# Two trunk layers of a diffusion backbone: the FFN's gate and up products by Strassen's seven products

## The chip, the cores and the metric

The kernel runs on one core of a Trainium2 chip. A core has TensorE (PE, matrix products; PEld is its weight loads), VectorE (DVE), ScalarE (ACT) and GpSimd (POOL); SyncE (SP) issues most DMAs. The metric is device time in microseconds of one launch. The kernel before takes 1474.19 us, the median of three runs (1473.52 to 1476.16).

## The reference, cut to what matters

640 tokens (128 of a prompt, 512 of a sample) of width 1024 pass two layers. Layer 0 mixes by attention and a state-space scan, layer 1 by pooling. Each layer ends with the same dense FFN, and each of its two halves has a norm ahead and a gated residual behind it:

```python
D_FF = 2816
def swiglu(h, w_gate, w_up, w_down):
    return (jax.nn.silu(h @ w_gate) * (h @ w_up)) @ w_down

for l in range(2):
    ...                                    # mixer, residual
    fp = swiglu(modulate(xp, norm_pre_ffn[l], shf_p, scf_p), ffn_w_gate[l], ffn_w_up[l], ffn_w_down[l])
    xp = xp + gf_p * rmsnorm(fp, norm_post_ffn[l])   # and the same for xs
```

Everything is float32.

## The kernel before, in words

**Products.** A float32 product is made of three fp32r matmuls: both operands are split into a rounded high part and a low part (x minus high), and high x high, high x low and low x high are summed in PSUM (mm3, lines 87 to 93; the three groups L91, L92, L93 of the profile). ACT makes each high part, DVE or POOL each low part. For weights this is `unit` (lines 79 to 85): a DMA of 128 x 1024 into a `raw` buffer (a ring of four), `wh` by ACT, `wl` by DVE.

**FFN.** The width of 2816 is 22 tiles (ft) of 128. Gate and up of one ft: `wproj` (line 382) and `whalf` (line 375) run 8 k-blocks x 3 matmuls over each half of 320 tokens: 24 matmuls of 320 columns into one PSUM bank. ACT applies Silu to the gate (L386), DVE multiplies by up (L389), ACT and POOL split the result into `ah` and `al` (L390, L391). The ft are taken in parts of 2, 4, 4, 4, 4, 4 (PARTS); behind each part the down product of that part is added to `y` in SBUF: per token tile tt (five of 128) and half dh (512 columns) 3 matmuls of 512 columns per ft, and one DVE addition (L446; ACT's copy L444 in the first part).

**Start of an FFN.** The tiles tt leave the mixer one by one: post-norm and residual (post_half L339, L340, postnorm L354), pre-norm (L300, L303 or L305), eight PE transposes (L315), evacuation with scale and shift (L320 on DVE, L322 on ACT), split into `hh` and `hl` (L328, L329). The first part uses a cut at 384 tokens: PE can run on tiles 0 to 2 while tiles 3 and 4 (called tails) are finished.

**Background.** The residual gates come from a product of one vector with `w_mod`. `mod_gate_mac` does it on DVE: 16 multiply-adds of 512 columns (L269) per half of a gate. Three gates of two halves, 96 multiply-adds, are mixed into the FFNs through `bg()`, which runs one step between products.

**Order.** Every engine runs its own instructions in order. A scheduler lays that order when the program is built; a queued instruction waits for its inputs and holds all behind it on its engine.

Of the kernel before, what the change touches and what calls it, by code (L numbers as in the profile page):

```python
# [9 lines left out]
F32 = mybir.dt.float32  # L10
F32R = mybir.dt.float32r
# [16 lines left out]
CUT = 384  # L28
SCALE = (64 + 32) ** -0.5
PARTS = [2, 4, 4, 4, 4, 4]  # L30
KEYS = 768
LAG = 2
BAL = ((0, 0, 4), (0, 0, 0), (1, 0, 0))
# [14 lines left out]
class Net:  # L48
# [205 lines left out]
    def mod_gate_mac(self, gt, l, j, half, gain):  # L254
# [20 lines left out]
        for v in range(2):  # L275
# [9 lines left out]
            nc.vector.tensor_tensor(gt[:, v, c0 : c0 + 512], out, gb, ALU.mult)  # L285
            yield

    def mod_gate(self, pool, l, j, gain, mac=True):
        gt = pool.tile([P, 2, D], F32, tag="G", name=self.name("G"))
        f = self.mod_gate_mac if mac else self.mod_gate_half  # L290
        self.bgq += [f(gt, l, j, half, gain) for half in range(2)]
        return gt

    def prenorm(self, x, tt, ab, hh=None, hl=None, full=None, bal=(0, 0, 0)):
# [12 lines left out]
        def tr():  # L307
            f = full
            if f is None:
                f = self.work.tile([P, KC, P], F32, tag="full", name=self.name("full"), bufs=1)  # L310
            for q in range(2):
# [21 lines left out]
    def post_half(self, y, dst, tt, g, half, ss=None):  # L333
# [4 lines left out]
        dump = self.work.tile([P, 512], BF16, tag="dump", name=self.name("dump"), bufs=1)  # L338
# [43 lines left out]
    def ffn(self, l, xs, hh, hl, g, fp, mk_y, tails, after):  # L382
        nc, t = self.nc, self.t

        def gate(cs, s, og):
            nc.scalar.activation(s[:, cs], og, AF.Silu)  # L386

        def up(s, cs, ou, ah, al):
            nc.vector.tensor_tensor(s[:, cs], s[:, cs], ou, ALU.mult)  # L389
            nc.scalar.activation(ah[:, cs], s[:, cs], AF.Copy)  # L390
            nc.gpsimd.tensor_tensor(al[:, cs], s[:, cs], ah[:, cs].bitcast(F32), ALU.subtract)  # L391

        def tiles():
            s = fp.tile([P, TOK], F32, tag="sg", name=self.name("sg"), bufs=2)
            ah = fp.tile([P, TOK], F32R, tag="ah", name=self.name("ah"), bufs=4)
            al = fp.tile([P, TOK], F32R, tag="al", name=self.name("al"), bufs=4)
            return s, ah, al

        ft = 0
        for pi, cnt in enumerate(PARTS):  # L400
            lastp = pi == len(PARTS) - 1
            at = []
            if pi == 0:
                us = [
                    self.unit(t[w][l, f], 1024, nc.gpsimd)
                    for f in range(cnt) for w in ("w_gate", "w_up")
                ]
# [1059 lines left out]
```

## Time and profile before

| | |
|---|---|
| time, median of 3 | 1474.19 us |
| span of the profiled execution, first to last instruction | 1471.5 us |
| PE busy | 1408.8 us, 96% |
| DVE / ACT / POOL busy | 745.0 (51%) / 534.6 (36%) / 240.1 (16%) us |
| mean granted TensorE clock | 0.983 of full |
| read from HBM | 146.14 MB, 102 GB/s over the span |

The profiled execution shows its span; 1474.19 - 1471.5 = 2.7 us of the median lie around it. Busy times of PE are modelled and overlap, so the distance between the starts of matmuls tells more than their length. An engine's idle time matters where it holds another up.

### The profile page before, as it was taken

To read this page: it belongs to the slowest core of one execution; us is meant where nothing else is said; L and a number is where in the kernel's file an instruction comes from. 1 tells how busy PE (TensorE), PEld (TensorE's weight loads), DVE (VectorE), ACT (ScalarE), POOL (GpSimd) and SP (SyncE) were. 2 spreads that over 40 slices of the span, in tenths; PEclk is the share of its full clock that TensorE was granted. 3 is DMA by queue.
4 is the path that set the end of the run, shared out by engine and by line. 5 is a ranking of instruction groups with operands and counts; after the bars stand their busy time and mean duration, and the time that the engine had idled before them with its cause. 6 is when DMAs were issued, how large, how long until landed. Compare 5 with 4: busy or idle time off the path is not lost.

```text
span 1471.5 us, 20386 instructions
## 1 busy us (share of the span) xinstructions
PE 1408.8 (96%) x8256; PEld 1220.3 (83%) x8256; DVE 745.0 (51%) x1200; ACT 534.6 (36%) x1003; POOL 240.1 (16%) x243
## 2 busy tenths in 40 slices
PE   5999999999998999999999999769999999999998
PEld 2888764677566999998989999659998989999996
DVE  4755548777747425636633232895255432322326
ACT  3544635744225432221222222676321222222223
POOL 0000144344303101011211102211120101101010
PEclk9999999999999999999999999989999999999999
DMA  9433445500351223334422222101242312222211
GB/s 366 134 129 126 142 145 189 188 30 1 114 171 59 80 72 129 112 109 137 137 72 72 72 86 72 58 29 65 86 131 93 129 57 87 73 86 72 72 44 72
DMA packets 46217, 150.74 MB, mean 102 GB/s; under 512 B 5606, under 2 KB 9190, under 8 KB 46124
## 3 DMA queue, kind: packets, MB, share of 16 engines
q1 hardware_dynamic: 40176, 143.48, 28.6%
q10 hardware_dynamic: 5948, 5.97, 1.3%
q8 instruction: 65, 1.06, 0.3%
q14 instruction: 28, 0.23, 0.1%
HBM read 146.14 MB, written 3.29 MB: 102 GB/s over the span
## 4 chain that ended last, share of the span: by engine, by line
PE 87%; DVE 6%; ACT 3%; issue 2%; DMA 2%; POOL 0%; ACTq 0%; DVEq 0%; POOLq 0%
PE ps L91 25%; PE ps L92 25%; PE ps L93 25%; PE ps L175 3%; PE ps L1001 1%; DVE xs L354 1%; DVE hl L329 1%; PE ps L809 1%; PE ps L963 1%; PE ps L983 1%; PE ps L984 1%; PE ps L986 1%; PE ps L985 1%; DVE pw L1102 1%; ACT full L322 0%
## 5 line engine op out<-in xcount | busy, mean ns | idle before, releaser
L91 PE MATMUL ps<-hh,wh 128*128 128x320 f32 (+3 forms) x1616 | 501.2, 310 | 7.5 <-DVE hh L328 7.1
L92 PE MATMUL ps<-hl,wh 128*128 128x320 f32 (+3 forms) x1616 | 498.7, 309 | 2.6 <-DVE hl L329 2.6
L93 PE MATMUL ps<-hh,wl 128*128 128x320 f32 (+3 forms) x1616 | 498.4, 309 | 0.0
L84 DVE TENSOR_TENSOR wl<-raw,wh 128x1024 fp32r<-128x1024 f32 (+1 forms) x153 | 189.3, 1239 | 284.2 <-ACT wh L83 283.9
L91 PEld LDWEIGHTS ps<-hh,wh 128*128 128x128 f32 (+1 forms) x1616 | 303.1, 188 | 20.0 <-DVE hh L328 7.3
L83 ACT ACTIVATE wh<-raw 128x1024 fp32r<-128x1024 f32 (+1 forms) x161 | 170.1, 1058 | 411.1 <-PE ps L92 204.6
L92 PEld LDWEIGHTS ps<-hl,wh 128*128 128x128 f32 (+1 forms) x1616 | 303.0, 188 | 4.6 <-DVE hl L329 3.6
L93 PEld LDWEIGHTS ps<-hh,wl 128*128 128x128 f32 (+1 forms) x1616 | 302.9, 187 | 0.4 <-DVE wl L84 0.3
L391 POOL TENSOR_TENSOR al<-sg,ah 128x320 fp32r<-128x320 f32 (+2 forms) x88 | 112.2, 1274 | 726.6 <-ACT ah L390 726.6
L92 PE MATMUL ps<-wl,ah 128*128 128x512 f32 x440 | 172.9, 393 | 0.0
L91 PE MATMUL ps<-wh,ah 128*128 128x512 f32 x440 | 172.3, 392 | 0.0
L93 PE MATMUL ps<-wh,al 128*128 128x512 f32 x440 | 171.6, 390 | 0.0
L389 DVE TENSOR_TENSOR sg<-sg,ps 128x320 f32<-128x320 f32 (+2 forms) x88 | 42.8, 487 | 160.3 <-PE ps L93 160.3
L446 DVE TENSOR_TENSOR y<-y,ps 128x512 f32<-128x512 f32 x100 | 68.5, 685 | 104.0 <-PE ps L93 103.9
L91 PEld LDWEIGHTS ps<-wh,ah 128*128 128x128 f32 x440 | 82.6, 188 | 18.3
L93 PEld LDWEIGHTS ps<-wh,al 128*128 128x128 f32 x440 | 82.6, 188 | 18.1
L92 PEld LDWEIGHTS ps<-wl,ah 128*128 128x128 f32 x440 | 82.7, 188 | 16.8
L390 ACT ACTIVATE ah<-sg 128x320 fp32r<-128x320 f32 (+2 forms) x88 | 40.8, 463 | 110.3 <-DVE sg L389 110.2
L386 ACT ACTIVATE sg<-ps 128x320 f32<-128x320 f32 (+2 forms) x88 | 37.7, 428 | 98.5 <-PE ps L93 98.5
L269 DVE SCALAR_TENSOR_TENSOR macc<-raw,silc,macc 128x512 f32<-128x512 f32 x84 | 62.4, 792 | 5.3 <-DMA raw<-in_w_mod 5.3
L175 PE MATMUL ps<-raw,silc 128*32 128x512 f32 x224 | 55.5, 613 | 0.3 <-DMA raw<-in_w_mod 0.3
L315 PE MATMUL ps<-cm,junk 128*128 128x128 f32 x120 | 18.8, 308 | 19.9 <-DVE junk L305 11.8
(305 smaller groups left out, 1629.1 us busy)
## 6 DMA issues: line engine op xcount, KB each, us to landing
raw<-in_w_mod SPq DMA_DIRECT2D x80, 512.0 KB, 3.4
raw<-in_w_gate SPq DMA_DIRECT2D x44, 512.0 KB, 3.2
raw<-in_w_up SPq DMA_DIRECT2D x44, 512.0 KB, 3.3
raw<-in_w_down SPq DMA_DIRECT2D x44, 512.0 KB, 3.3
mraw<-in_w_mod SPq DMA_DIRECT2D x16, 512.0 KB, 6.4
raw<-in_w_xbc SPq DMA_DIRECT2D x8, 512.0 KB, 4.3
raw<-in_w_out SPq DMA_DIRECT2D x8, 512.0 KB, 4.7
x<-in_x_sample SPq DMA_DIRECT2D x4, 512.0 KB, 9.2
```

Source lines behind the costliest of these rows:

```text
L83: self.nc.scalar.activation(h[:, :n], x[:, :n], AF.Copy)
L84: (eng or self.nc.vector).tensor_tensor(l[:, :n], x[:, :n], h[:, :n].bitcast(F32), ALU.subtract)
L91: mm(out, ah, bh, start=first and i == 0, stop=False)
L92: mm(out, ah, bl, start=False, stop=False)
L93: mm(out, al, bh, start=False, stop=last and i == n - 1)
L175: nc.tensor.matmul(out[32 * g : 32 * g + 32], self.silc[:, kc], x[:, k2 * 512 : k2 * 512 + 512], start=kc < 4, stop=kc >= 4,)
L269: nc.vector.scalar_tensor_tensor(acc[:, v], x[:, k2 * 512 : k2 * 512 + 512], self.silc[:, kc, v : v + 1], acc[:, v] if kc else bb, op0=ALU ...
L386: nc.scalar.activation(s[:, cs], og, AF.Silu)
L389: nc.vector.tensor_tensor(s[:, cs], s[:, cs], ou, ALU.mult)
L390: nc.scalar.activation(ah[:, cs], s[:, cs], AF.Copy)
L391: nc.gpsimd.tensor_tensor(al[:, cs], s[:, cs], ah[:, cs].bitcast(F32), ALU.subtract)
L446: nc.vector.tensor_tensor(yd, yd, out, ALU.add)
```

## The change

Gate and up of a pair of ft (256 columns) become one 2x2 block product: the contraction is cut in two halves of 512, the columns in two ft, the tokens in two halves of 320. Strassen's scheme in the form of Winograd needs seven block products instead of eight, and sums of blocks ahead of and behind them. A block product is 4 k-blocks x 3 matmuls of 320 columns.

- Weights (`Matrix`): per pair and matrix two `raw` tiles, four POOL subtractions of 512 columns (`adds`), and four splits: a (the raw tile itself, products p1, p2), c (p5, p6), b (p7, p3), d (p4, 512 columns).
- Activations (`Halves`): `take` splits tokens 0 to 319 as before (`a1`). From tile 3 on `pair` forms the four sums S1 to S4 of the halves (three on DVE, one on POOL) and splits them and the block A22 (`a2`). p1 and p2 read only a1, all other products a2.
- Results: the PSUM tile A is carried through p1, p6, p7, p4 and copied out by ACT in between; B holds p5 and p3; DVE adds them up in SBUF.
- Down product: per pair of ft, five tiles of six matmuls, placed between products by `d()`, each with a DVE addition; `d()` also runs one background step. The last two pairs are kept for the end.
- The residual x and the three gates go to scratch in DRAM and are read back at the end of each FFN, which frees SBUF for a2.

```diff
-PARTS = [2, 4, 4, 4, 4, 4]
+NPAIR = NFT // 2
...
-BAL = ((0, 0, 4), (0, 0, 0), (1, 0, 0))
...
+    def split(self, pool, tag, x, eng=None):
+        n = x.shape[1]
+        h = pool.tile([P, n], F32R, tag="h" + tag, name=self.name("h" + tag))
+        l = pool.tile([P, n], F32R, tag="l" + tag, name=self.name("l" + tag))
+        self.nc.scalar.activation(h, x, AF.Copy)
+        (eng or self.nc.vector).tensor_tensor(l, x, h.bitcast(F32), ALU.subtract)
+        return h, l
...
+    def take(self, tt):
+        nc = self.net.nc
+        if tt < 3:
+            cs = slice(tt * P, min(tt * P + P, HB))
+            h, l = (a[:, :, cs] for a in self.a1)
+            x = self.f[:, :, cs]
+            nc.vector.tensor_copy(h, x)
+            nc.vector.tensor_tensor(l, x, h.bitcast(F32), ALU.subtract)
+        if tt == 3:
+            self.pair(0, 64)
+        if tt >= 3:
+            self.pair(tt * P - HB, P)
+
+    def pair(self, c0, n):
+        nc = self.net.nc
+        cs = slice(c0, c0 + n)
+        fa, fb = self.f[:, :, cs], self.f[:, :, HB + c0 : HB + c0 + n]
+        t = self.tmp.tile([P, 4, 4, P], F32, tag="st", name=self.net.name("st"))[:, :, :, 0:n]
+        h, l = self.a2
+        s1, s2 = t[:, self.S1], t[:, self.S2]
+        nc.vector.tensor_tensor(s1, fb[:, 0:4], fb[:, 4:8], ALU.add)
+        nc.gpsimd.tensor_tensor(t[:, self.S3], fa[:, 0:4], fb[:, 0:4], ALU.subtract)
+        nc.vector.tensor_tensor(s2, s1, fa[:, 0:4], ALU.subtract)
+        nc.vector.tensor_tensor(t[:, self.S4], fa[:, 4:8], s2, ALU.subtract)
+        for i in range(2):
+            b = slice(2 * i, 2 * i + 2)
+            self.split(
+                h[:, b, :, cs].rearrange("p s k c -> p (s k) c"),
+                l[:, b, :, cs].rearrange("p s k c -> p (s k) c"),
+                t[:, b].rearrange("p s k c -> p (s k) c"), nc.vector,
+            )
+        self.split(h[:, self.A22, :, cs], l[:, self.A22, :, cs], fb[:, 4:8], nc.gpsimd)
...
+    def load(self):
+        self.ra = self.net.raw(self.src[2 * self.pair])
+        self.rb = self.net.raw(self.src[2 * self.pair + 1])
+
+    def adds(self):
+        g = self.net.nc.gpsimd
+        lo, hi = slice(0, 512), slice(512, 1024)
+        self.q = self.fr.tile([P, 1024], F32, tag="q", name=self.net.name("q"))
+        self.t4 = self.fr.tile([P, 512], F32, tag="t4", name=self.net.name("t4"))
+        g.tensor_tensor(self.q[:, lo], self.rb[:, lo], self.ra[:, lo], ALU.subtract)
+        g.tensor_tensor(self.q[:, hi], self.rb[:, hi], self.q[:, lo], ALU.subtract)
+        g.tensor_tensor(self.rb[:, lo], self.rb[:, hi], self.rb[:, lo], ALU.subtract)
+        g.tensor_tensor(self.t4, self.ra[:, hi], self.q[:, hi], ALU.subtract)
...
+        terms = [t for k in range(4) for t in ((wh, bh, k), (wh, bl, k), (wl, bh, k))]
+        for n, (x, z, k) in enumerate(terms):
+            mm(out, x[:, k], z[:, k], start=first and n == 0, stop=n == len(terms) - 1, skip_group_check=True)
...
+        def p1(self):
+            self.A = net.pt([P, HB])
+            self.m.product(self.A, 1, A, True, True)
+            nc.scalar.activation(self.blk(0, 0), self.A, AF.Copy)
+
+        def p2(self):
+            c = net.pt([P, HB])
+            self.m.product(c, 2, A, True, True)
+            nc.vector.tensor_tensor(self.blk(0, 0), self.blk(0, 0), c, ALU.add)
+            self.act(0, 0)
+
+        def p6(self):
+            self.m.product(self.A, 6, A, False, True)
+            nc.scalar.activation(self.blk(1, 0), self.A, AF.Copy)
+
+        def p5(self):
+            self.B = net.pt([P, HB])
+            self.m.product(self.B, 5, A, True, True)
+
+        def p7(self):
+            self.m.product(self.A, 7, A, False, True)
+            nc.scalar.activation(self.blk(1, 1), self.A, AF.Copy)
+            nc.vector.tensor_tensor(self.blk(1, 1), self.blk(1, 1), self.B, ALU.add)
+
+        def p4(self):
+            self.m.product(self.A, 4, A, False, True)
+            self.act(0, 1, self.A)
+
+        def p3(self):
+            self.m.product(self.B, 3, A, False, True)
+            nc.vector.tensor_tensor(self.blk(1, 0), self.blk(1, 0), self.B, ALU.add)
+            if self.g is None:
+                nc.scalar.activation(self.s[:, 1], self.s[:, 1], AF.Silu)
             else:
-                us = [[dunit(j, dh) for j in range(cnt // 2)] for dh in range(2)]
-                lag = []
-                for tt in range(NT):
-                    y2 = [y[:, tt, dh * 512 : dh * 512 + 512] for dh in range(2)]
-                    down(tt, 0, us[0])
-                    self.bg()
-                    u = self.post_tile()
-                    ss = self.post_half(y2[0], u[0], tt, g, 0)
-                    down(tt, 1, us[1])
-                    self.bg()
-                    if len(lag) >= LAG:
-                        lag.pop(0)()
-                    self.post_half(y2[1], u[1], tt, g, 1, ss)
-                    if l == 0:
-                        self.postnorm(u, ss, xs[:, tt])
-                        lag.append(after(tt))
-                    else:
-                        self.postnorm(u, ss, xs[:, tt], lambda cs: after(tt, cs))
-            ft += cnt
-        return lag
+                nc.vector.tensor_tensor(self.g.s[:, 1], self.g.s[:, 1], self.s[:, 1], ALU.mult)
...
+        def d():
+            if fill:
+                down_add(fill.pop(0), up, [(prev, wdn)], p == 1)
+            net.bg()
+
+        if nx and n != 0:
+            nx.load()
+        if n >= 2:
+            w.p1()
+            w.p2()
+        if final and up:
+            last[1, 0] = net.split(fr, "a", down_load(NPAIR - 1, 0), None)
+        w.p6()
+        d()
+        w.p5()
+        if nx and n != 0:
+            nx.a()
+        w.p7()
+        if nx:
+            nx.adds()
+        d()
+        if nx:
+            nx.c()
+        if final and up:
+            last[0, 1] = net.split(fr, "c", down_load(NPAIR - 2, 1), None)
+        w.p4()
+        if up:
+            at = [out_split(wg, 0)]
+        d()
+        w.p3()
+        if up:
+            at.append(out_split(wg, 1))
+        if nx:
+            nx.b()
+            nx.d()
+        d()
+        d()
+        if up:
+            if final:
+                last[1, 1] = net.split(fr, "b", down_load(NPAIR - 1, 1), None)
+                last["at"] = (prev, at)
+            prev = at
+        if nx and 1 <= n and (n + 1) // 2 < NPAIR - 1:
+            wdn = net.split(fr, "w", down_load((n + 1) // 2 - 1, (n + 1) % 2), None)
...
-            lag.append(net.prenorm(xs[:, tt], tt, ab_ffn, hh, hl, bal=BAL[0]))
+            x = xq.pop(0)
+            net.postnorm([y[:, tt, 0:512], u[1]], sss[tt], x)
+            nc.sync.dma_start(xd[0, tt], x)
+            if tt + 3 < NT:
+                x_in(tt + 3)
+            lag.append(net.prenorm(x, tt, ab_ffn, sink=A, bal=(0, 4)))
...
+    def x_back(pl, k):
+        xs = pl.tile([P, NT, D], F32, name=net.name("xs"))
+        for tt in range(NT):
+            nc.sync.dma_start(xs[:, tt], xd[k, tt])
+        return xs
```

**Where instructions move.** On DVE at the start of the first FFN, from the evacuation of tile 3 to that of tile 4 (`full` is the evacuated tile, `xs` the residual, `sg` the gate), before:

```order
L320 TENSOR_SCALAR full_4490<-ps_4500,mv_418,mv_417 128x128
L354 SCALAR_TENSOR_TENSOR xs<-ymix,r_4416,xs 128x512
L354 SCALAR_TENSOR_TENSOR xs<-junk_4411,r_4416,xs 128x512
L320 TENSOR_SCALAR full_4490<-ps_4500,mv_418,mv_417 128x128 x3
L328 CAST hh_3853<-full_4490 128x8x128
L329 TENSOR_TENSOR hl_3854<-full_4490,hh_3853 128x8x128
L99 RECIPROCAL r_4425<-sd_4424 128x1
L305 TENSOR_SCALAR junk_4421<-xs,r_4425 128x1024
L389 TENSOR_TENSOR sg_4458<-sg_4458,ps_4511 128x384
L320 TENSOR_SCALAR full_4539<-ps_4549,mv_418,mv_417 128x128 x4
L328 CAST hh_3853<-full_4539 128x8x128
L329 TENSOR_TENSOR hl_3854<-full_4539,hh_3853 128x8x128
```

After, the last tile's part (`st` the sums, `a2l` low parts of a2, `la`, `lw` low parts of weights for later products):

```order
L433 TENSOR_TENSOR st_4535<-full_3857 128x512
L526 TENSOR_TENSOR sg_4490<-sg_4490,sg_4491 128x320
L435 TENSOR_TENSOR st_4535<-st_4535,full_3857 128x512
L90 TENSOR_TENSOR la_4752<-raw_4721,ha_4751 128x1024
L436 TENSOR_TENSOR st_4535<-full_3857,st_4535 128x512
L411 TENSOR_TENSOR a2l_4463<-st_4535,a2h_4462 128x8x128
L90 TENSOR_TENSOR lw_4825<-raw_4822,hw_4824 128x1024
L411 TENSOR_TENSOR a2l_4463<-st_4535,a2h_4462 128x8x128
L433 TENSOR_TENSOR st_4593<-full_3857 128x512
L435 TENSOR_TENSOR st_4593<-st_4593,full_3857 128x512
L436 TENSOR_TENSOR st_4593<-full_3857,st_4593 128x512
L411 TENSOR_TENSOR a2l_4463<-st_4593,a2h_4462 128x8x128 x2
```

One cast and one low part per tile have become three sums and two low parts, and the low parts of weights stand between them.

On ACT at the start of the second FFN, before (`full` again the evacuations of tiles 3 and 4):

```order
L98 ACTIVATE sd_8841<-ss_8839,eps 128x1
L322 ACTIVATE full_8902<-ps_8903,mv_1564,mv_1565 128x128
L303 ACTIVATE junk_8838<-xs,r_8842 128x1024
L322 ACTIVATE full_8902<-ps_8903,mv_1564,mv_1565 128x128 x3
L322 ACTIVATE full_8902<-ps_8912,mv_1564,mv_1565 128x128 x4
L390 ACTIVATE ah_8871<-sg_8870 128x384
L322 ACTIVATE full_8951<-ps_8952,mv_1564,mv_1565 128x128 x4
L322 ACTIVATE full_8951<-ps_8961,mv_1564,mv_1565 128x128 x4
L386 ACT_TABLE_LOAD
```

After, from the first high parts of a2 (`ha`, `hw` are high parts of later weights):

```order
L410 ACTIVATE a2h_9127<-st_9189 128x8x64 x2
L410 ACTIVATE a2h_9127<-full_8730 128x4x64
L410 ACTIVATE a2h_9127<-full_8730 128x4x128
L523 ACT_TABLE_LOAD
L523 ACTIVATE sg_9155<-sg_9155 128x320
L410 ACTIVATE a2h_9127<-st_9200 128x8x128 x2
L531 ACTIVATE sg_9156<-ps_9226 128x320
L335 ACTIVATE full_8730<-ps_9240,mv_1571,mv_1572 128x128 x4
L335 ACTIVATE full_8730<-ps_9249,mv_1571,mv_1572 128x128 x4
L89 ACTIVATE ha_9416<-raw_9386 128x1024
L410 ACTIVATE a2h_9127<-full_8730 128x4x128
L89 ACTIVATE hw_9489<-raw_9487 128x1024
L410 ACTIVATE a2h_9127<-st_9258 128x8x128 x2
```

The evacuation of tile 4 (ps_9240, ps_9249) now stands behind the table load and four high parts, and behind it come two high parts of weights ahead of tile 4's own.

On DVE in the stretch where a gate is computed, before (`macc` is the gate's sum, `wl` low parts):

```order
L389 TENSOR_TENSOR sg_4938<-sg_4938,ps_5030 128x320
L269 SCALAR_TENSOR_TENSOR macc_5340<-raw_5341,silc,macc_5340 128x512
L84 TENSOR_TENSOR wl_5248<-raw_5245,wh_5247 128x1024
L269 SCALAR_TENSOR_TENSOR macc_5340<-raw_5375,silc,macc_5340 128x512 x4
L269 SCALAR_TENSOR_TENSOR macc_5340<-raw_5409,silc,macc_5340 128x512
L84 TENSOR_TENSOR wl_5312<-raw_5309,wh_5311 128x1024
L269 SCALAR_TENSOR_TENSOR macc_5340<-raw_5409,silc,macc_5340 128x512 x2
L389 TENSOR_TENSOR sg_5061<-sg_5061,ps_5128 128x320
L269 SCALAR_TENSOR_TENSOR macc_5340<-raw_5409,silc,macc_5340 128x512
L389 TENSOR_TENSOR sg_5061<-sg_5061,ps_5153 128x320
L84 TENSOR_TENSOR wl_5318<-raw_5315,wh_5317 128x1024
```

After, in one matrix of layer 0:

```order
L275 SCALAR_TENSOR_TENSOR macc_5390<-raw_5391,silc,bb_5385 128x512
L526 TENSOR_TENSOR sg_5208<-sg_5208,sg_5399 128x320
L90 TENSOR_TENSOR la_5470<-raw_5400,ha_5469 128x1024
L590 TENSOR_TENSOR y<-y,ps_5446 128x512
L275 SCALAR_TENSOR_TENSOR macc_5390<-raw_5391,silc,macc_5390 128x512 x2
L275 SCALAR_TENSOR_TENSOR macc_5390<-raw_5503,silc,macc_5390 128x512
L90 TENSOR_TENSOR lc_5506<-q_5487,hc_5505 128x1024
L550 TENSOR_TENSOR sg_5399<-sg_5399,ps_5456 128x320
L275 SCALAR_TENSOR_TENSOR macc_5390<-raw_5503,silc,macc_5390 128x512
L590 TENSOR_TENSOR y<-y,ps_5493 128x512
L275 SCALAR_TENSOR_TENSOR macc_5390<-raw_5503,silc,macc_5390 128x512 x2
L526 TENSOR_TENSOR sg_5208<-sg_5208,ps_5404 128x320
```

The multiply-adds are the same ones; between them now stand the low parts of four weight blocks instead of two units, the block additions and the additions to y.

## Rows read from the trace of the kernel before

**Rows 1.** Page, part 1: busy time, share and instructions of each engine.
```profile
PE 1408.8 (96%) x8256; PEld 1220.3 (83%) x8256; DVE 745.0 (51%) x1200; ACT 534.6 (36%) x1003; POOL 240.1 (16%) x243
```

**Rows 2.** Groups by shape, TensorE: count | busy us, mean ns | idle.
```profile
L91 PE MATMUL ps<-hh,wh 128*128 128x320 f32 x1472 | 455.6, 310 | 0.0
```

**Rows 3.** Timeline, TensorE in layer 0's FFN: start, length in us.
```profile
560.33 0.31 PE L91 MATMUL ps<-hh,wh 128*128 128x320 f32 x1
...
563.41 0.31 PE L91 MATMUL ps<-hh,wh 128*128 128x320 f32 x1
...
599.62 0.39 PE L91 MATMUL ps<-wh,ah 128*128 128x512 f32 x1
...
603.97 0.39 PE L92 MATMUL ps<-wl,ah 128*128 128x512 f32 x1
```

**Rows 4.** Windows of the FFN: stretch, busy us and count of each engine.
```profile
640.00:720.00 80.00, 80.00 (x476) 74.72 (x475) 48.77 (x66) 18.93 (x29) 10.38 (x7) 1.00 0.37 124
720.00:800.00 80.00, 80.00 (x477) 74.88 (x477) 26.62 (x34) 19.05 (x29) 10.09 (x8) 1.00 0.26 87
```

**Rows 5.** Groups by shape, VectorE (DVE).
```profile
L84 DVE TENSOR_TENSOR wl<-raw,wh 128x1024 fp32r<-128x1024 f32 x152 | 188.4, 1241 | 284.2 <-ACT wh L83 283.9
L446 DVE TENSOR_TENSOR y<-y,ps 128x512 f32<-128x512 f32 x100 | 68.5, 685 | 104.0 <-PE ps L93 103.9
L269 DVE SCALAR_TENSOR_TENSOR macc<-raw,silc,macc 128x512 f32<-128x512 f32 x84 | 62.4, 792 | 5.3 <-DMA raw<-in_w_mod 5.3
L389 DVE TENSOR_TENSOR sg<-sg,ps 128x320 f32<-128x320 f32 x80 | 38.9, 487 | 146.8 <-PE ps L93 146.8
L279 DVE TENSOR_TENSOR modl<-macc,modh 128x512 fp32r<-128x512 f32 x12 | 8.2, 684 | 0.3
```

**Rows 6.** Groups by shape, GpSimd (POOL).
```profile
L391 POOL TENSOR_TENSOR al<-sg,ah 128x320 fp32r<-128x320 f32 x80 | 102.0, 1275 | 668.8 <-ACT ah L390 668.8
L1018 POOL TENSOR_TENSOR cal<-a,cah 128x512 fp32r<-128x512 f32 x4 | 5.2, 1296 | 11.8 <-ACT cah L1017 11.8
L1232 POOL TENSOR_TENSOR csl<-zs,csh 128x640 fp32r<-128x640 f32 x4 | 6.1, 1554 | 20.3 <-ACT csh L1231 20.3
```

**Rows 7.** Groups by shape, ScalarE (ACT).
```profile
L83 ACT ACTIVATE wh<-raw 128x1024 fp32r<-128x1024 f32 x160 | 169.4, 1060 | 411.1 <-PE ps L92 204.6 <-PE ps L93 115.7 <-issue 70.0
L322 ACT ACTIVATE full<-ps,mv,mv 128x128 f32<-128x128 f32 x60 | 22.9, 461 | 11.9 <-PE ps L315 5.9 <-DVE r L99 3.7 <-DVE hl L329 2.4
L98 ACT ACT_TABLE_LOAD x6 | 7.7, 1283 | 0.1
```

**Rows 8.** Timeline before the first FFN: VectorE, then GpSimd.
```profile
459.22 0.75 DVE L354 SCALAR_TENSOR_TENSOR xs<-ymix,r,xs 128x512 f32<-128x512 f32 x1
...
466.46 2.86 DVE L354 SCALAR_TENSOR_TENSOR xs<-ymix,r,xs 128x512 f32<-128x512 f32 x1
...
469.25 2.82 DVE L354 SCALAR_TENSOR_TENSOR xs<-junk,r,xs 128x512 f32<-128x512 f32 x1
...
475.79 3.38 DVE L329 TENSOR_TENSOR hl<-full,hh 128x1024 fp32r<-128x1024 f32 x1
...
465.50 8.79 POOL L84 TENSOR_TENSOR wl<-raw,wh 128x1024 fp32r<-128x1024 f32 x3 [58.68 <-ACT wh L83]
...
475.69 2.39 POOL L84 TENSOR_TENSOR wl<-raw,wh 128x1024 fp32r<-128x1024 f32 x1 [1.41 <-ACT wh L83]
```

**Rows 9.** Timeline of the same start, TensorE.
```profile
479.22 0.69 PE L92 MATMUL ps<-hl,wh 128*128 128x384 f32 x1 [1.00 <-DVE hl L329]
...
480.34 0.52 PE L92 MATMUL ps<-hl,wh 128*128 128x384 f32 x1
...
484.28 0.34 PE L92 MATMUL ps<-hl,wh 128*128 128x384 f32 x1
```

**Rows 10.** Timeline before the second FFN: TensorE, then VectorE.
```profile
999.96 0.44 PE L92 MATMUL ps<-hl,wh 128*128 128x384 f32 x1 [1.23 <-DVE hl L329]
...
1001.58 1.41 DVE L354 SCALAR_TENSOR_TENSOR xs<-junk,r,xs 128x512 f32<-128x512 f32 x2
```

More of the change, by code (lines that the diff above doesn't have):

```diff
@@ L307, in tr @@
         def tr():
-            f = full
-            if f is None:
-                f = self.work.tile([P, KC, P], F32, tag="full", name=self.name("full"), bufs=1)
+            f = sink.f[:, :, tt * P : tt * P + P] if full is None else full
             for q in range(2):
@@ new lines, with __init__, second, begin @@
+class Halves:
+    S2, S1, S3, S4, A22 = range(5)
+    def __init__(self, net, pool):
+        self.net = net
+        self.a1 = [pool.tile([P, KC, HB], F32R, name=n) for n in ("a1h", "a1l")]
+    def second(self, pool, tmp):
+        self.a2 = [pool.tile([P, 5, 4, HB], F32R, name=self.net.name(n)) for n in ("a2h", "a2l")]
+        self.tmp = tmp
+    def begin(self, pool):
+        self.f = pool.tile([P, KC, TOK], F32, name=self.net.name("full"))
+    def split(self, h, l, x, eng):
+        nc = self.net.nc
+        nc.scalar.activation(h, x, AF.Copy)
+        eng.tensor_tensor(l, x, h.bitcast(F32), ALU.subtract)
+    def take(self, tt):
[11 more added lines that the diff above has]
+    def pair(self, c0, n):
+        nc = self.net.nc
+        cs = slice(c0, c0 + n)
[15 more added lines that the diff above has]
+        self.split(h[:, self.A22, :, cs], l[:, self.A22, :, cs], fb[:, 4:8], nc.gpsimd)
+    def block(self, i):
+        if i < 2:
+            return [a[:, 4 * i : 4 * i + 4] for a in self.a1]
+        return [a[:, i - 2] for a in self.a2]
@@ L1079, in _pool_tile, with wt @@
     i0 = 8 - c0
[L1081 to L1084 removed]
+    def wt(g):
+        n = KC - 2 * (g % 2)
+        return pp.tile([P, n, 144], F32, tag=f"pw{g % 2}", name=net.name("pw"))
+    cur, at = wt(0), 0
     a, b = max(c0 - 7, 1), min(c0 + P + 7, n)
@@ L1263, in trunk @@
         us = {k: net.unit(t["w_out"][0, k]) for k in (2, 3, 0, 1)}
+        for tt in range(3):
+            x_in(tt)
         outs = [net.pt([P, 512]) for _ in range(NT)]
@@ new lines, in trunk, with finish_tiles @@
+    st = {}
+    def finish_tiles(tail, xs_of, g, after, out=None):
+        lag = []
+        for tt in range(NT):
+            y0 = tail(tt, 0)
+            net.bg()
+            u = net.post_tile()
+            ss = net.post_half(y0, u[0], tt, g, 0)
+            y1 = tail(tt, 1)
+            net.bg()
+            if len(lag) >= LAG:
+                lag.pop(0)()
+            net.post_half(y1, u[1], tt, g, 1, ss)
+            if out:
+                net.postnorm(u, ss, xs_of(tt), lambda cs: out(tt, cs))
+            else:
+                net.postnorm(u, ss, xs_of(tt))
+                lag.append(after(tt))
+        return lag
@@ new lines, in x_back, with finish0, after @@
+    def x_back(pl, k):
+        xs = pl.tile([P, NT, D], F32, name=net.name("xs"))
+        for tt in range(NT):
+            nc.sync.dma_start(xs[:, tt], xd[k, tt])
+        return xs
+    def gates0():
+        net.mod_gate_store(gd[0], 0, 5, "npost_ffn")
+        net.mod_gate_store(gd[1], 1, 2, "npost_mix")
+    ts = ExitStack()
+    def finish0(tail, right):
+        xs = st["xs"] = x_back(ts.enter_context(pool("xs", "left")), 0)
+        g = net.gate_load(right, gd[0])
+        st["g1"] = net.gate_load(ts.enter_context(pool("gp", "left")), gd[1])
+        net.work = net.dp = ts.enter_context(pool("workt", "left", 2))
+        def after(tt):
+            if tt == 0:
+                st["ab"] = net.mod_ab_of(1, m1[0], m1[1], PV_PREMIX)
+                st["abf"] = net.mod_ab_of(1, m1[3], m1[4], PV_PREFFN)
+                st["hf"] = ts.enter_context(pool("hfp", "left")).tile([P, KC, TOK], F32, name="hf")
+            return net.prenorm(xs[:, tt], tt, st["ab"], full=st["hf"][:, :, tt * P : tt * P + P])
+        return finish_tiles(tail, lambda tt: xs[:, tt], g, after)
```

333 lines of the change are left out of this document (192 added, 141 removed).

## The prediction

> **What bounds the kernel now.** I read the page's busy times first, then the groups of TensorE by shape, then timelines of the FFN and of the two places where an FFN starts. The reader should see three things. TensorE is busy 96% of the span [rows 1], and in the middle of an FFN it never waits: 80.00 of 80.00 us at full clock, with and without a gate being computed [rows 4]. There a matmul costs its distance to the next one: 21 starts of 320 columns lie between 560.33 and 563.41, so 0.1467 us each; 19 starts of 512 columns between 599.62 and 603.97, so 0.229 us [rows 3]. The lengths of 310 ns in the groups [rows 2] overlap and are not the cost. DVE, ACT and POOL only feed TensorE: DVE has 48.8 of 80 us of work while a gate is computed and 26.6 of 80 otherwise [rows 4]. TensorE does wait where an FFN starts: in the first one the stream of matmuls becomes dense at 479.22 after a wait for the low part of tile 2, and then runs at half clock for a while (0.52 us a piece at 480.34, 0.34 at 484.28) [rows 9]; in the second at 999.96, at full clock [rows 10].
>
> **What is removed.** Gate and up have 22 ft x 2 matrices x 2 halves x 24 = 2112 matmuls of 320 columns a layer, 4224 in two layers (the first part's cut at 384 and 256 columns has the same sum of columns). Seven products of 12 make 84 a matrix of two ft where 96 stood: 44 matrices x 12 = 528 matmuls fewer. At 0.1467 us that is **77.5 us off TensorE**, on the path throughout, since nothing else holds TensorE up there. The down product keeps its 1320 matmuls.
>
> **What is added in the steady state.** One matrix with its 30 down matmuls lasts 84 x 0.1467 + 30 x 0.229 = 19.2 us on TensorE. In that time:
> - DVE: low parts a, b, c and the down weights 4 x 1.24, d 0.68, three additions from PSUM 1.46, five additions to y 3.43, products gate x up about 0.9 on average: 11.4 us [rows 5].
> - POOL: four block subtractions of 512 columns at 1.30 and one low part of 640 at 1.55: 6.75 us [rows 6]; before, two pieces of 320, 2.55 us.
> - ACT: four high parts of 1024 at 1.06, and copies, about 8 us [rows 7].
>
> Each is far under 19.2, and every weight block is split about a matrix ahead, so outside the gates I charge 2 us in all (0 to 10). With a gate, 96 multiply-adds at 0.79 [rows 5] with their splits come on top, spread over 12 matrices in layer 0 and 6 in layer 1. Counted through the new order with the durations above, DVE's own work there is 15.4 us a matrix on average and 20.4 in the four heaviest.
>
> What the sums hide is that DVE and POOL do not work side by side. While POOL made three low parts (465.50 to 474.29), two residual updates on DVE took 2.86 and 2.82 us instead of 0.75; a low part that began 0.1 us after a POOL one took 3.38 [rows 8]. So POOL's 6.75 us can be lost to DVE wholly or in part. The part depends on how often DVE wants two SBUF inputs at that moment, and POOL's mean of 1.275 us for 320 columns beside 1.30 for 512 [rows 6] says that POOL too stands and waits. I take half: 15.4 + 3.4 = 18.8 of 19.2 on average, and in the four heavy matrices 20.4 + 3.4 - 19.2 = 4.6 us too much, of which the PSUM tiles and early weights swallow about 3. With some spill into their neighbours: 9 us (0, if DVE hides it, to 32; full loss would be 18 x 6.75 + 272 - 18 x 19.2 = 48, less what runs beside additions from PSUM, a third).
>
> The Trainium skill ("SBUF — State Buffer", section "Who interferes with whom") states this as a rule: GpSimd and a VectorE instruction with two SBUF inputs share an exclusive lock, and the later one stands until the earlier has ended, while a VectorE instruction with one SBUF input goes on. The three stretched pieces agree with it. Taken to the letter it gives the third rival below; half a loss gives my sum.
>
> **The start of the first FFN** is the dearest place. p1 and p2 of gate and up need only tokens 0 to 319; that is 48 matmuls, 7.0 us. Every other product needs a2, which is complete only after the last tile's sums and splits. The three POOL low parts no longer stand in front of the residual updates (2 x 2.1 us), so the first products begin at about 475.5 instead of 479.2. From there DVE must run, in its order: the residual of tile 4 (1.6), three weight low parts (3.7), d (0.7), two tiles' evacuations (8 x 0.38 = 3.0), a scaling (0.8), nine sums (six of 512 at 0.69, three of half that, 5.3), six low parts of a2 (two of 512, four of 1024: 6.3), three pieces for p2 (1.5): 22.9 us, to 498.4. POOL has about 19 us of pieces in the same stretch; I take 8 of them as lost. p6 needs all but the last low part, so it starts near 505 rather than at 486 to 490, where TensorE runs dry. Restarting at half clock costs 1.8: before, it lasted from 479.2 to a point between 480.34 and 484.28 [rows 9], I take 3.7 us, half of them lost. The delay is 505 + 1.8 - 475.5 - 7.0 = 24.3, against 479.2 + 1.8 - 475.5 = 5.5 before: **19 us lost** (11 with no collision, 28 with all).
>
> **The start of the second FFN.** Tile 4's residual ends at 1001.58 + 1.4 = 1003 [rows 10]. ACT then has, in order: its square, the evacuation of tile 3 and a scaling (1.3 + 2.9 + 1.4), four high parts for the first 64 and 128 columns (2.2), a table load 1.28 and Silu 0.4, two high parts and a copy (2.5), the evacuation of tile 4 (2.9), three pieces of 1.06, 0.6 and 1.06, and the first high part of tile 4 (1.1): 18.7 us [rows 7], to 1021.7. DVE adds two low parts, 2.5: p6 at 1024.2, with collisions 1026. The delay is 1026 + 1.8 - 7.0 against 999.96 + 1.6 for tails' transposes: **19 us lost** (14 to 24). What hid the tails before, 96 matmuls of 384 columns, has become 48 of 320.
>
> **Smaller pieces.** The pooling stage, bound by DVE before 1000, gets POOL's first subtractions and three low parts beside it: 3 (0 to 6). In the first and last pair of each FFN no down product stands between p7 and p4, so p4 waits for ACT's copy of A, about 0.4 and a hand-over, eight times: 4 (2 to 8). The last split of each FFN is one of 640 instead of 320 columns: 2 (0 to 5). The read-back of x (5 x 512 KB) starts when the last product frees a2 and has two down tiles and a post-norm as cover; stores of x and gates have no reader near: nothing, and up to 5 in the bound if it is late.
>
> **Sum.** -77.5 + 2 + 9 + 19 + 19 + 3 + 4 + 2 = -19.5 us against the profiled execution: span 1452.0, and with the 2.7 us around it 1454.7. The median of the runs has the same 2.7, so I predict **1455 us**.
>
> **Rivals.**
> 1. *A clean win.* The ends of the starts are the low ones (11 + 14), gates are hidden, and the small pieces cost 5: -77.5 + 30 = -47.5, 1427. For it: DVE, ACT and POOL are half idle in every FFN window [rows 4]. Against: ACT's chain at the second start has no slack in it.
> 2. *A's bank is handed over late.* A is written four times and copied by ACT in between; if the down tile (6 x 0.229 = 1.4 us) does not cover a copy that stands behind a 1.06 us high part, each matrix pays about 0.7 more: 44 x 0.7 = 31, and the change gives nothing like its eighth: 1486. Against: the copy stands ahead of the c split in ACT's order.
> 3. *The lock decides (slower).* POOL's pieces stand wholly in DVE's way. Then DVE needs 15.4 + 6.75 = 22.1 of 19.2 us in 18 matrices, 48 us with TensorE waiting for low parts and for sums of B, and the starts cost 28 + 24; with 5 elsewhere 105 in all: 1502. It turns slower than before from a total of 77.5 us of cost on: with the starts at 38 and 11 us elsewhere that is 28 us in the gate stretches, where over four fifths of POOL's time stops DVE; with dear starts, half. For it: the rows on the collision, and four subtractions in a row that return after every DVE piece.
>
> **Chances.** My forecast 0.48 (its own range 1438 to 1472), the clean win 0.20, late hand-over 0.10, the lock 0.22. The range that leaves out two in ten runs from 1424 to 1500. A measurement of this kernel tells about 0.2%, 3 us, from no change: faster by more 0.66 (nearly all of the first two), within 0.06, slower 0.28.
>
> **What would show it.** Right: 528 matmuls fewer, at the same 0.1467 us between starts; a wait of TensorE of 14 to 20 us before the first product with a2 in each layer, ended by a low part of a2 on DVE, and half clock behind it; full clock and nearly no wait from the third matrix on; short waits where `macc` runs. Wrong: a wait in every matrix ended by ACT (second rival) or by DVE low parts with DVE near 100% busy and pieces stretched by POOL's (third); no wait at the starts (first).

## The result, and the profile after

Before, 1475.16 us (median of 4 runs); after, 1484.16 us (4 runs, 1481.71 to 1486.1). The ratio is 1.0062, with a 95% interval from 1.0044 to 1.008: the change makes the kernel slower by 0.6%. I had forecast 1455. The profiled execution has a span of 1479.9 us against 1471.5, so 8.4 us more have to be found in the trace, and with the 77.5 us that TensorE no longer needs, some 86 us of new cost.

The page after, busy time and instructions (answers to [rows 1]):

```profile
PE 1353.1 (91%) x7728; PEld 1152.2 (78%) x7728; DVE 1041.8 (70%) x1502; ACT 662.5 (45%) x1173; POOL 479.5 (32%) x385
```

The 528 matmuls are gone (8256 to 7728). VectorE has 297 us more and GpSimd twice what it had. The same two windows as in [rows 4], in the first FFN with a gate being computed:

```profile
640.00:720.00 80.00, 78.58 (x460) 72.13 (x460) 69.76 (x84) 30.93 (x44) 28.55 (x17) 1.00 0.36 112
720.00:800.00 80.00, 77.92 (x449) 71.97 (x448) 62.28 (x74) 30.54 (x43) 39.33 (x24) 0.98 0.36 114
```

Before, TensorE was busy 80.00 of 80.00 in both. Now it stands, though VectorE (fourth number) is not full. The two places where an FFN meets its first product with a2, timeline of TensorE (start, length, in brackets the idle time ahead and what ended it):

```profile
507.25 0.90 PE L497 MATMUL ps<-a2h,hc 128*128 128x320 f32 x2 [16.19 <-ACT a2h L410]
...
1035.91 0.90 PE L497 MATMUL ps<-a2h,hc 128*128 128x320 f32 x2 [12.42 <-ACT a2h L410]
1039.10 0.63 PE L497 MATMUL ps<-a2l,hc 128*128 128x320 f32 x1 [2.29 <-DVE a2l L411]
```

I took every distance between starts of neighbouring matmuls less the distance of the dense stream (0.1467 us for 320 columns, 0.229 for 512). What is over is a wait where one distance is long, and slow running where a whole row of them is stretched (half clock). In us:

| stretch of the program | before: wait, slow | after: wait, slow | more |
|---|---|---|---|
| first FFN's start (450 to 530) | 9.2, 3.2 | 28.4, 5.1 | 21 |
| rest of it (to 920; 924) | 0, 0 | 14.3, 7.7 | 22 |
| pooling stage (to 999.9; 1011.5) | 22.6, 15.8 | 28.2, 18.4 | 8 |
| second FFN's start (to 1050) | 0.6, 0 | 16.5, 3.4 | 19 |
| rest of it | 0, 0 | 9.9, 4.6 | 15 |

Together 85, and with 0.5 elsewhere less 77.5 the 8 us of the span. The starts cost what was forecast; the surprise is in the middle of the FFNs. One turn of a pair there, the timelines of VectorE, GpSimd, ScalarE and TensorE, in this order:

```profile
526.77 3.04 DVE L275 SCALAR_TENSOR_TENSOR macc<-raw,silc,bb 128x512 f32<-128x512 f32 x2 [1.75 <-DMA raw<-in_w_mod]
...
530.39 0.48 DVE L526 TENSOR_TENSOR sg<-sg,ps 128x320 f32<-128x320 f32 x1
...
532.56 1.38 DVE L562 TENSOR_TENSOR sg<-sg,sg 128x640 f32<-128x640 f32 x1
533.87 2.59 DVE L90 TENSOR_TENSOR lb<-raw,hb 128x1024 fp32r<-128x1024 f32 x1
536.39 0.47 DVE L536 TENSOR_TENSOR sg<-sg,ps 128x320 f32<-128x320 f32 x1
...
538.87 4.06 DVE L275 SCALAR_TENSOR_TENSOR macc<-raw,silc,macc 128x512 f32<-128x512 f32 x6
...
526.26 1.30 POOL L468 TENSOR_TENSOR q<-raw,q 128x512 f32<-128x512 f32 x1
527.52 1.74 POOL L469 TENSOR_TENSOR raw<-raw 128x512 f32<-128x512 f32 x1
...
531.61 1.65 POOL L470 TENSOR_TENSOR t<-raw,q 128x512 f32<-128x512 f32 x1 [1.22 <-DVE ld L90]
533.23 4.63 POOL L568 TENSOR_TENSOR al<-sg,ah 128x640 fp32r<-128x640 f32 x2
...
530.90 0.74 ACT L567 ACTIVATE ah<-sg 128x640 fp32r<-128x640 f32 x1 [3.75 <-DVE sg L526]
531.54 1.04 ACT L89 ACTIVATE hb<-raw 128x1024 fp32r<-128x1024 f32 x1
532.49 0.42 ACT L531 ACTIVATE sg<-ps 128x320 f32<-128x320 f32 x1
...
532.96 0.41 PE L497 MATMUL ps<-a2h,hc 128*128 128x320 f32 x1 [1.69 <-ACT sg L531]
...
537.92 0.50 PE L99 MATMUL ps<-hw,al 128*128 128x512 f32 x1 [1.51 <-POOL al L568]
...
538.89 0.47 PE L497 MATMUL ps<-a2h,hc 128*128 128x320 f32 x1
...
541.29 0.47 PE L497 MATMUL ps<-a2h,hb 128*128 128x320 f32 x1
```

Read it from TensorE upward. The first product with a2 waits for ScalarE's copy of A (L531). That copy needs only p1, but in ScalarE's order it stands behind `ah` and `hb`, and `ah` waited 3.75 us for VectorE's product gate x up (L526, 530.39). VectorE was behind: ahead of that product stood multiply-adds of a gate, which waited 1.75 us for their weights from DRAM; the first two then took 3.04 us beside GpSimd's subtractions, where six of them later took 4.06. Then TensorE waits a second time, for `al` on GpSimd: the two `al` stood behind a subtraction (531.61) and took 4.63 us, beside VectorE's product of 640 columns (1.38 us) and its low part lb (2.59 us). After these two waits TensorE runs at half clock, granted 0.50 of full (1.2 of 2.4 GHz) from 538.5 to 541.5: nine distances between the starts at 538.89 and 541.29 are 0.267 us each.

Sorted by whether a GpSimd piece overlapped them by over 0.15 us (440 us to the end), VectorE's pieces fall into two kinds. Two inputs in SBUF: ld, 0.69 us alone (20 pieces), 1.27 beside GpSimd (24); la, 1.22 alone (28), 1.87 beside (14); the product of 640, 0.81 alone (4), 1.72 beside (18). One input in SBUF and one in PSUM: additions to y, 0.68 alone (90), 0.68 beside (90). This is what the Trainium skill ("SBUF — State Buffer", section "Who interferes with whom") says of the shared ports, and the trace agrees to the piece: of the low parts of weights and of a2 (L90, L411), 72 began while a GpSimd tensor_tensor was running, and 71 of them took, within 0.15 us, what was left of that piece plus their own length alone. Another 24 were running when the GpSimd piece began, and took their length alone. So which of the two stands depends on which began first.

### The profile page after: what moved, and what is told of

It is laid out like the page before. It is cut to its first block, busy times and chain, and to the rows that moved or that the text cites. A ratio compares the mean times of both kernels' runs of the same rounds, so it can differ in the third digit from the quotient of the medians.

```text
span 1479.9 us, 20167 instructions
## 1 busy us (share of the span) xinstructions
PE 1353.1 (91%) x7728; PEld 1152.2 (78%) x7728; DVE 1041.8 (70%) x1502; ACT 662.5 (45%) x1173; POOL 479.5 (32%) x385
## 5 line engine op out<-in xcount | busy, mean ns | idle before, releaser
L99 PE MATMUL ps<-hw,al 128*128 128x512 f32 x380 | 150.3, 396 | 4.4 <-POOL al L568 4.4
L98 PE MATMUL ps<-lw,ah 128*128 128x512 f32 x380 | 150.4, 396 | 1.2 <-DVE lw L90 1.2
L97 PE MATMUL ps<-hw,ah 128*128 128x512 f32 x380 | 150.7, 396 | 0.0
L497 PE MATMUL ps<-a2h,hc 128*128 128x320 f32 x352 | 112.2, 320 | 38.0 <-ACT a2h L410 28.6
L497 PE MATMUL ps<-a2l,hc 128*128 128x320 f32 x352 | 112.0, 318 | 2.6 <-DVE a2l L411 2.6
L497 PE MATMUL ps<-a2h,lc 128*128 128x320 f32 x352 | 111.8, 319 | 0.0
L497 PE MATMUL ps<-a2h,lb 128*128 128x320 f32 x352 | 109.3, 311 | 0.0
L497 PE MATMUL ps<-a1h,ha 128*128 128x320 f32 x336 | 104.9, 312 | 4.9 <-DVE a1h L419 4.9
L497 PE MATMUL ps<-a2h,hb 128*128 128x320 f32 x352 | 109.0, 310 | 0.0
L497 PE MATMUL ps<-a2l,hb 128*128 128x320 f32 x352 | 108.8, 309 | 0.0
L90 DVE TENSOR_TENSOR lc<-q,hc 128x1024 fp32r<-128x1024 f32 x42 | 53.0, 1261 | 67.1 <-ACT hc L89 67.1
```

Source lines behind the costliest of these rows:

```text
L90: (eng or self.nc.vector).tensor_tensor(l, x, h.bitcast(F32), ALU.subtract)
L97: mm(out, ah, bh, start=first and i == 0, stop=False)
L98: mm(out, ah, bl, start=False, stop=False)
L99: mm(out, al, bh, start=False, stop=last and i == n - 1)
L497: mm(out, x[:, k], z[:, k], start=first and n == 0, stop=n == len(terms) - 1, skip_group_check=True)
```

## The experiments

The rivals: A, the gates' multiply-adds crowd VectorE; B, GpSimd's pieces hold VectorE up (the lock of the prediction's third rival); C, the order of the instructions itself is late. For the starts, theory S: TensorE lacks work that needs only a1. Each ratio is to runs of the kernel before on the same chip (median 1475.1 us for e1 to e4, 1473.9 for e5 to e8, 1474.5 for e9 to e12); the kernel after was 1484.2.

**e1, without multiply-adds.**
```
 for v in range(2):
+    if kc:
+        continue
     nc.vector.scalar_tensor_tensor(acc[:, v], ...
```


> This kernel leaves out 84 of the 96 multiply-adds of the gates computed during the two FFNs (the gate rows are the bias and the first 128 rows of the product only). Theory A, crowded VectorE: the multiply-adds make VectorE late at the turn of a pair, ScalarE's copy of A waits in order behind a split that waits for VectorE, TensorE stands about 2 us and then runs a while at half clock; about 31 us of the loss hang on it, so 1453 to 1460. Theory B, the lock: GpSimd's pieces stop VectorE with or without the multiply-adds; 8 to 15 us go, 1470 to 1476. Theory C, the order itself hands A over late: within 5 us of 1484.


Measured 1464.6 (ratio to before 0.993, 0.991 to 0.995): 20 us faster than after. Neither range was met: the multiply-adds are part of it, and not all.

**e2, the same multiply-adds over more matrices.**
```
+        steps = [1, 1, 1, 0, 0]
+
         def d():
...
-            net.bg()
+            net.bg(steps.pop(0))
```


> The whole computation; the gate's steps are taken at three of the five places of a matrix instead of all five, none in its last two, so the same multiply-adds are spread over 19 matrices instead of 11 in the first FFN and 10 instead of 6 in the second. Theory A: most of the waits in the gate stretches vanish, 15 to 25 us, 1459 to 1469. Theory B: the same pieces meet as often, within 5 us of 1484. Theory C: within 5 us of 1484.


Measured 1472.0 (0.998, 0.997 to 0.9995): 12 us faster than after, a gain smaller than A's and larger than B's. Fewer multiply-adds at a turn help; the waits for `al` stay.

**e3, block subtractions on VectorE.**
```
     def adds(self):
-        g = self.net.nc.gpsimd
+        g = self.net.nc.vector
```


> The four block subtractions of each weight matrix go from GpSimd to VectorE, nothing else. They cost VectorE 4 x 0.69 = 2.75 us a matrix there. Theory A (VectorE has too much work where the multiply-adds run, and the lock takes little): 5 to 15 us slower, 1489 to 1499. Theory B (GpSimd's subtractions cost VectorE more than they would take on it): 10 us or more faster, at most 1474. Theory C: within 5 us of 1484.


Measured 1447.8 (0.982, 0.979 to 0.984): 36 us faster than after. A fell and B stands. The groups by shape of after (busy us, mean ns):

```profile
L469 POOL TENSOR_TENSOR raw<-raw 128x512 f32<-128x512 f32 x44 | 68.5, 1557 | 0.0
...
L590 DVE TENSOR_TENSOR y<-y,ps 128x512 f32<-128x512 f32 x180 | 120.5, 680 | 47.0 <-PE ps L99 46.3
L275 DVE SCALAR_TENSOR_TENSOR macc<-raw,silc,macc 128x512 f32<-128x512 f32 x84 | 73.8, 915 | 4.2 <-DMA raw<-in_w_mod 4.2
L90 DVE TENSOR_TENSOR ld<-t,hd 128x512 fp32r<-128x512 f32 x44 | 44.2, 1005 | 31.5 <-ACT hd L89 30.4
L562 DVE TENSOR_TENSOR sg<-sg,sg 128x640 f32<-128x640 f32 x22 | 34.3, 1558 | 0.7
```

And the same groups of e3:

```profile
L469 DVE TENSOR_TENSOR raw<-raw 128x512 f32<-128x512 f32 x44 | 30.0, 683 | 0.0
...
L590 DVE TENSOR_TENSOR y<-y,ps 128x512 f32<-128x512 f32 x180 | 121.0, 681 | 34.3 <-PE ps L99 33.6
L275 DVE SCALAR_TENSOR_TENSOR macc<-raw,silc,macc 128x512 f32<-128x512 f32 x84 | 62.8, 780 | 0.0
L90 DVE TENSOR_TENSOR ld<-t,hd 128x512 fp32r<-128x512 f32 x44 | 31.1, 706 | 11.7 <-ACT hd L89 11.6
L562 DVE TENSOR_TENSOR sg<-sg,sg 128x640 f32<-128x640 f32 x22 | 21.8, 990 | 0.5
```

A subtraction takes 0.68 us on VectorE and 1.56 on GpSimd. VectorE got 124.9 us of them (four such groups) and its busy time rose by 21.7 only, from 1041.8 to 1063.5: 103 us of its busy time had been standing beside GpSimd's subtractions. The windows of e3:

```profile
640.00:720.00 80.00, 80.00 (x474) 74.58 (x473) 73.80 (x107) 31.47 (x45) 8.29 (x6) 1.00 0.38 126
720.00:800.00 80.00, 79.58 (x469) 73.70 (x468) 65.61 (x91) 32.46 (x45) 7.43 (x5) 1.00 0.33 106
```

VectorE shows more busy time than after, and between 525 and 905 TensorE waits only once, 0.4 us. The starts are as they were:

```profile
505.99 0.90 PE L497 MATMUL ps<-a2h,hc 128*128 128x320 f32 x2 [16.02 <-ACT a2h L410]
...
1013.82 0.90 PE L497 MATMUL ps<-a2h,hc 128*128 128x320 f32 x2 [12.38 <-ACT a2h L410]
```

**e4, the first pair of each FFN by eight products** (core of the edit; the sums follow afterwards):
```
-    wg.p1()
+    wg.std(0, 0)
     tails.pop(0)()
-    wg.p2()
-    wu.p1()
+    wg.std(1, 0)
+    wu.std(0, 0)
     tails.pop(0)()
-    wu.p2()
+    wu.std(1, 0)
+    for w in (wg, wu):
+        for f in range(2):
+            w.std(f, 1)
+    A.sums()
```
With it the first pair needs no block subtractions, and the low parts of A22 go from GpSimd to VectorE.

> The whole computation; the first pair of gate and up tiles of each FFN by the eight products, 48 matmuls more in all (7 us), so that 96 instead of 48 matmuls need only the first 320 tokens; the sums for the second half are made afterwards. Theory S (TensorE's waits of 16.4 and 12.6 us before the first product with a2 are what the starts cost): the waits shrink to 3 to 6 us each, and with the 7 us more of matmuls 12 to 18 us are gained, 1466 to 1472. Rival (the chain of VectorE is what is long, and the wait comes back at the second pair): within 5 us of 1484.


Measured 1455.2 (0.987, 0.984 to 0.989): 29 us faster than after, more than S asked. TensorE, where its first product with the second half stands in each FFN:

```profile
493.87 0.41 PE L560 MATMUL ps<-l,ha 128*128 128x320 f32 x1 [1.55 <-DVE l L434]
...
1008.45 0.63 PE L560 MATMUL ps<-h,ha 128*128 128x320 f32 x1 [2.57 <-ACT h L433]
```

16.2 and 12.4 us became 1.6 and 2.6. A part came back at the second pair, as the rival had it: its first product with a2 waits 3.9 us at 515.21 and 3.6 at 1031.39. By the same count of distances, taken between the same matmuls, the two starts with the second pair gained 31 us less the 7 of matmuls, and the pooling stage 7, where the subtractions for the second FFN's first pair had stood beside VectorE; the gate stretches lost 4. The 2 us that are left of the difference of the profiles lie ahead of the first FFN.

**e5, only `al` on VectorE.**
```
-        nc.gpsimd.tensor_tensor(al, g.s[:, f], ...
+        nc.vector.tensor_tensor(al, g.s[:, f], ...
```


> The changed kernel with one edit: the low parts of the gated products (al, 44 of 640 columns) go from GpSimd to VectorE, the block subtractions stay on GpSimd. The run before showed that the subtractions on GpSimd cost 36 us; two ways remain in which they could. B1 (they stretch VectorE's pieces): VectorE gets 44 x 0.85 = 37 us more work and the stretching stays, so within 8 us of 1484. B2 (they stand in GpSimd's queue ahead of al, for which TensorE waits in four places): the waits ended by al go, 10 to 20 us faster, 1464 to 1474.


Measured 1480.7 (1.0045, 1.003 to 1.006), 3.5 us faster than after: B1. The waits ended by `al` did go, as B2 had it (4.9 us to 0.5 between 525 and 930), but while the subtractions stay on GpSimd, TensorE's waits for ScalarE's copies of A grow there from 7.2 us to 10.8 (5.3 before p6 and 5.5 before p4), and little is gained.

**e6, e3 and e4 together.**


> The whole computation; both edits together: block subtractions on VectorE, and the first pair of each FFN by eight products. With the subtractions moved, the two waits at the starts were as long as ever (16.2 and 12.5 us), so the two gains should add: 1447.8 - 29 = 1419, between 1415 and 1425. If VectorE becomes the bound where the sums for the second half now stand, 1430 or more.


Measured 1429.8 (0.970, 0.968 to 0.972). The gains don't add in full, 54 of 65 us by the medians. Counted in the profiles from the 2451st matmul on, ahead of the first FFN, they are 35.7 and 26.7 alone and 56.8 together, so 5.6 us are in both. They lie in the pooling stage: from the last pair's `al` to the last pooling product after takes 87.1 us, e3 81.6, e4 80.4, and both together 80.3.

**e7, e6 with `al` on VectorE.**


> As e6_adds_std1, with the low parts of the gated products on VectorE too, so that GpSimd has next to nothing in an FFN. If GpSimd's remaining 44 pieces still cost VectorE more than it needs for them itself: 4 to 10 us faster than e6. If VectorE is full where the multiply-adds run (74 of 80 us): 5 to 15 us slower than e6.


Measured **1414.9** (0.961, 0.958 to 0.964): 15 us faster than e6, more than the 4 to 10 expected, and 4% faster than the kernel before. Of the 17.0 us between the two profiled spans 6.4 lie ahead of the first FFN, which no edit touches (the 2451st matmul starts at 461.4 in e6 and 455.0 in e7; at 456.2 in after); 10.6 are the edit's. Its windows:

```profile
640.00:720.00 80.00, 80.00 (x473) 74.48 (x472) 75.22 (x112) 32.98 (x47) 0.00 (x0) 1.00 0.39 129
720.00:800.00 80.00, 80.00 (x473) 74.39 (x472) 61.22 (x87) 32.04 (x44) 0.00 (x0) 1.00 0.29 93
```

TensorE is dense at full clock with VectorE at 75 of 80 us: so much load is no bound by itself.

**e8, e6 with the last pair's `al` on VectorE.**


> As e6_adds_std1, with only the last pair's two low parts of each FFN on VectorE. In the first FFN TensorE waits 3.3 us for such a low part and then runs some 20 us at a lower clock, so 4 to 8 us faster than e6 if the wait goes; within 2 us if the half clock comes from the stretch of weak work behind it anyway.


Measured 1423.5 (0.965, 0.963 to 0.967): 6.3 us faster than e6. The wait of 3.2 us for `al` before the last down products is gone, 2.1 us for lb stand there instead, and the 30 us behind run at a granted clock of 1.00 instead of 0.94.

**e9, after with subtractions and `al` on VectorE**, seven products throughout.


> The changed kernel with seven products in every pair, but all of the FFN's work of GpSimd on VectorE: the block subtractions and the low parts al. If GpSimd's pieces are the cause of the waits in the gate stretches and of the wait at the last pair, and the starts are a matter of their own: 1447.8 less the 10 to 17 us that the same second edit gave with the first pair by eight products, 1431 to 1438. If the second edit only helped because the first pair was changed: within 4 us of 1447.8.


Measured 1441.6 (0.978, 0.975 to 0.981): 43 us faster than after, 6 us beyond e3, so less than I had expected but beyond the other bound. In the two middles, where after loses 36.5 us to waits and half clock, 5 are left; the waits at the starts stay (17.0 and 12.6).

**e10, e11: controls on the kernel before**, the edits of e5 and e1.


> The kernel before, with its low parts al (80 of 320 columns) on VectorE instead of GpSimd. TensorE never waits in the middle of its FFNs, so moving GpSimd's pieces can give nothing there: within 3 us of 1474. If the comparison above owes part of its gain to an edit that would have helped the kernel before as much: 10 us or more faster.

> The kernel before without 84 of the 96 multiply-adds of the FFNs' gates (left out of the computation). If the multiply-adds cost only where VectorE is late: within 3 us of 1474, where the changed kernel gained 20 us. If they cost in any kernel: 10 us or more faster.


Measured 1473.9 (0.9996, 0.998 to 1.001) and 1475.0 (1.000, 0.9985 to 1.0014): nothing. Where TensorE waits for nothing [rows 4], neither costs anything, so what e5 and e1 show of the kernel after is nothing that these edits would have given the kernel before as well.

**e12, the kernel before with the down product per pair.**
```
-PARTS = [2, 4, 4, 4, 4, 4]
+PARTS = [2] * 11
```


> The kernel before with one part of the change alone: the down product per pair of ff tiles instead of per four, which adds 100 additions to y of 0.685 us on VectorE and doubles the turns from up to down. If VectorE's spare time takes them and the low part al is in time: within 5 us of 1474. If each turn waits for al of the pair just made (1.3 us on GpSimd behind a product and a high part): 22 turns of some 2 us, 30 to 50 us slower.


Measured 1486.9 (1.008, 1.006 to 1.011): 12 us slower, between the two. TensorE has no wait from 530 to 920; some 9 of the 12 us lie where the first FFN ends and the pooling stage runs. There the last down products, which cover the post-norm, are half as many; that this is the reason is argued from the code. The changed kernel keeps two pairs for its last down products.

## Why the prediction was wrong, point by point

- *-77.5 us off TensorE*: right, 528 matmuls fewer at the same distances.
- *The two starts, 19 + 19*: right in place and size (21 and 19), and in cause with two slips. What TensorE's long wait ended with was ScalarE's high part of a2 (in the first FFN behind VectorE's sums), not a low part on VectorE. And the first products did not become dense at 475.5 but at 478.96, hardly earlier than before: GpSimd's three low parts (473.02 to 481.1) still met VectorE there, and the low part of a1 that TensorE waited for took 2.90 us instead of 0.68. e3 and e9 leave the waits as they were, e4 moves a part of them to the second pair, e7 has 1.6 and 2.6 us left.
- *Pooling stage 3*: 8. It holds 4.2 us of slow running behind the wait for the last pair's `al`, and e3 and e4 take 5.5 and 6.7 back; both take GpSimd's subtractions for the first pair out of this stage.
- *Gate stretches 9, the p4 copies 4, the steady state 2, the last split 2*: **17 forecast, 36.5 found. This is the step that failed**, and most of the 28 us by which the span (1479.9) missed its forecast (1452.0). Half a loss of GpSimd's time to VectorE was about right: over 18 matrices I took 61 us, and between 530 and 760 and between 1050 and 1165 VectorE's pieces were 54 us longer than their shortest of the same shape. What was wrong is the step behind it, that only what exceeds 19.2 us a matrix reaches TensorE and that PSUM tiles and early weights swallow most of that. VectorE was busy 193.5 of the 230 us and 91.6 of the 115 us of these stretches, standing included, so by that rule next to nothing would have reached TensorE. A matrix is no store: at each turn of a pair the product, `ah`, the copy of A and `al` follow one another across three queues, and a VectorE piece stretched there is late at once, however idle VectorE is later. e7 shows it from the other side, with 75 of 80 us and no wait.
- *Half clock*: I charged 1.8 us at each start and nothing elsewhere. In the middles it cost 12 us, behind waits of 1.0 to 3.4 us.
- *Late hand-over of A (first 0.7 us in every matrix, 31 in all)*: the mechanism exists, seven waits of 1.6 to 2.2 us for a copy of A, but only where VectorE is behind, not in every matrix. They come to 13.7 us of the 31; that the rival's 1486 is the number nearest to 1484.2 is luck. *The lock decides (1502)*: the right cause with too high a price; with 28 us in the gate stretches it was to turn slower, and the total was 86 of the 105. I gave it 0.22, since I counted it as load. (Its 48 us rest on 272 us of VectorE's own work; 18 x 15.4 is 277, which makes them 53.)
- *The order itself*: not the cause on TensorE and ScalarE. In e9, from 440 us on, 5340 of TensorE's 5353 matmuls and 725 of ScalarE's 757 instructions stand in the sequence that they have in after, and 5 us are lost in the middles in place of 36.5. VectorE's order did shift with the moved pieces (850 of the other 983 keep their sequence); no run holds it fixed.

What stays open: `al` on VectorE gives 10.6 us with the first pair by eight products (e6 to e7, by the profiles and without what lies ahead of the FFN) and 6.7 without (e3 to e9, counted alike). And no run took away the half clock alone, so its 20 us more (5.1 + 7.7 + 18.4 + 3.4 + 4.6 against 3.2 + 15.8) are read from the traces only.

## What to carry to other kernels

Before giving work to GpSimd beside a VectorE that feeds TensorE, look at what VectorE does at that moment: if it has two inputs in SBUF, up to the whole length of the GpSimd piece can be lost to it (here 103 us of standing for 261 us of subtractions). Compare with what VectorE would need itself (0.68 against 1.3 to 1.6 us a piece, 125 us in all). Price a loss at the hand-overs, queue by queue, and not against the mean load of a period. And where an algorithm needs all of its input at once, let its first tile go the plain way: 48 matmuls more bought 27 us (e9 to e7).

## What the hardware showed beyond that

Both engines pay: GpSimd's subtractions took 1.43 to 1.56 us on average, where 512 columns had taken 1.30 [rows 6], and two `al` beside VectorE's lows 4.63 us instead of twice 1.55. A piece with one SBUF input was held too, where the prediction's summary of the rule has such a piece go on: `junk<-x,r`, a tensor_scalar of 1024 columns, took 0.75 us alone and 2.86 us at 473.22, while GpSimd made low parts. The summary left out what the Trainium skill ("SBUF — State Buffer", section "Who interferes with whom") excepts: VectorE's two-port modes, which a tensor_scalar can enter, contend with GpSimd too. The trace agrees with that here.
